# Splitting float32 weights and activations in a two-layer decoder trunk: GpSimd's share of the weights goes to VectorE, feature-major tiles are split two at a time, and the idle products at the layer norms have other forms

## The chip, the cores and the metric

The kernel runs on one core of a Trainium2 chip. The core has TensorE (PE, matrix products, weight loads shown apart as PEld), VectorE (DVE), ScalarE (ACT), GpSimd (POOL) and SyncE (SP, which here only issues DMAs). Each engine runs its own instructions in order and waits for the others by semaphores. The metric is device time in microseconds (us) of one execution; lower is better. TensorE's clock has two levels, 2.4 and 1.2 GHz; the profile calls the first a granted clock of 1.00 and the second 0.50.

## The reference

Two post-norm decoder layers over 256 tokens of width 2048, all in float32, cut to the parts that give the work its order:

```python
for layer in range(2):
    mixed = even_mixer(x, ...) if layer == 0 else odd_mixer(x, ...)   # x @ w_in, attention, y @ w_out
    x = layer_norm(ALPHA * x + mixed, ln1_g[layer], ln1_b[layer])
    hid = jax.nn.relu(x @ mlp_w1[layer])                               # 2048 -> 8192
    x = layer_norm(ALPHA * x + (hid * hid) @ mlp_w2[layer], ln2_g[layer], ln2_b[layer])
```

The even mixer is a sliding-window attention beside a mixture of dilated ones, the odd mixer a stick-breaking attention beside a latent attention. Some 395 MB of weights are read once each.

## The kernel before

**Split products.** A float32 product is made of three products of numbers in the type float32r: each operand is split into a high part (a cast) and a low part (the operand less its high part). In the text *hi* and *lo* are these parts.

**Weights.** The class `Stream` holds all weights in the order of their use, in *units* of at most 128 x 1024 numbers (two k-tiles of 512 columns, for the products that matter here). SP loads a unit into one of 6 buffers `raw`, at least 5 units ahead; `_split` makes `w_hi` (ACT, L128) and `w_lo` (L129), 3 units ahead of the product, in 4 buffers each. So ACT can cast a new unit only when PE has finished with the unit four places before it. At the program's start and after each layer norm (`self.shared = SHARED`, 10) the next ten units are cut at column 320: ACT casts the two pieces one after the other, DVE subtracts the first 320 columns and GpSimd the other 704 (or 544).

**Activations.** x is kept token-major in `x_res`. `transposed` makes the feature-major k-tiles on demand, two at a time (a *pair*): four transposes on PE into one bank (L506), then for each of the two tiles ACT's copy with gain and bias into `xfull` (L516 or L518), DVE's cast to the high part (L519) and DVE's subtraction for the low part (L520). `LazyTiles.need` calls it just ahead of the unit that uses the pair: PE's order is pair 0, pair 1, unit 0, pair 2, unit 1, pair 3 and so on to pair 7, unit 6, unit 7. `xfull` has 3 buffers of 256 columns, and `join` (L345, L346), which adds the two sums of a bank, takes them too.

**The layer norm.** `layer_norm` ends a block: DVE adds the last column block to x for token tile 0, takes the moments, GpSimd raises the variance to the power -1/2 (`rs`, L559), and the same for token tile 1. PE has nothing to do then and `keep_clock` gives it products that nothing reads (L533). `z` (L584) normalizes x in place on DVE, 512 columns of one token tile at a time: the first block ahead of pair 0, the others behind pairs 0, 2 and 4. There are three such turns with products behind them, called here by layer and norm: turn (0, 1), turn (0, 2) and turn (1, 1). The last norm goes to the output.

**Work beside the products.** After each unit `pump` does one step of side work. One such step is in `x_new`, which multiplies the normed x by the gain and adds the bias; behind the norm with `ln == 2` it loads the gain and bias rows 128 columns at a time on GpSimd's queue (`g_row`, `b_row`), `lead` = 3 steps ahead in 4 buffers, and at the other norms whole (`gb_rows`). The first pumps of the program also issue the small loads (`gb`, `rg`, `masks`, `sinks`, L471) on GpSimd's queue.

The order on every engine is that in which the program is written; nothing reorders it.

Of the kernel before, what the change touches and what calls it, by code (L numbers as in the profile page):

```python
# [11 lines left out]
F32 = mybir.dt.float32  # L12
F32R = mybir.dt.float32r
# [5 lines left out]
P = 128  # L19
# [13 lines left out]
SHARED, DVE_PART = 10, 320  # L33
# [34 lines left out]
class Stream:  # L68
    """Weights in the order of their use: DMA ahead, split ahead into two float32r parts.
    For the next shared units GpSimd takes a share of the second part."""  # L70

    def __init__(self, k):
        self.k = k
        self.units = []
        self.nd = 0
        self.ns = 0
        self.nu = 0
        self.live = {}
        self.shared = SHARED
# [19 lines left out]
    def _split(self, upto):  # L99
        nc = self.k.nc  # L100
        while self.ns < min(upto, len(self.units)):
# [17 lines left out]
            else:  # L119
                m = n * width  # L120
                rv = raw.rearrange("p k c -> p (k c)")
                cuts = (0, m)
                if self.shared:
                    self.shared -= 1
                    cuts = (0, DVE_PART, m)
                pieces = [(hi[:, a:b], lo[:, a:b], rv[:, a:b]) for a, b in zip(cuts, cuts[1:])]
            for i, (h, l, r) in enumerate(pieces):
                nc.scalar.copy(h, r)  # L128
                (nc.gpsimd if i and perm is None else nc.vector).tensor_tensor(l, r, h.bitcast(F32), op=ALU.subtract)  # L129
# [14 lines left out]
class LazyTiles:  # L144
    """feature-major k-tiles that are made when a product comes near them"""
# [13 lines left out]
class Job:  # L159
    """one group of attention heads: scores, then stages of the weighting, then the values"""  # L160
# [11 lines left out]
class Trunk:  # L172
# [22 lines left out]
    # ---- work beside the products: one step per unit of weights  # L195
# [17 lines left out]
    def queue(self, job, u=None):  # L213
        """all heads; pattern u only, when the patterns come one by one"""
        if u is None:
            self.todo.extend((job, h, 0) for h in range(job.n))
        else:
            self.todo.extend((job, h, u) for h in range(job.n))
# [42 lines left out]
    def flip(self, job, h, u):  # L261
        """weights of a head (and pattern) to keys-major"""
# [40 lines left out]
    # ---- psum  # L303
# [3 lines left out]
    # ---- matrix products; xs: per k-tile (hi, lo) of [128, 256]  # L307
# [4 lines left out]
    def ws(self, xs, nkt, width, take, more=False):  # L312
        """weights stationary, feature-major result. Per 128 features one bank: the first 256 columns sum
        hi x hi, the other 256 the two cross terms; take(f, bank) is called when the sums of tile f are complete"""
# [26 lines left out]
    def join(self, out, bank, scale=1.0):  # L341
        """both sums of a bank, scaled by a power of two"""
        nc = self.nc
        t = self.small.tile([P, S], F32, name="xfull", bufs=3)
# [3 lines left out]
    def as_(self, xs, nkt, width, hold=0):  # L348
        """activations stationary: token-major result [128 tokens, width] for both token tiles;
        the last hold units of weights serve first the one token tile, then the other"""  # L350
# [35 lines left out]
    # ---- weights in the order in which the products below take them  # L386
# [58 lines left out]
    # ---- set-up  # L445
# [49 lines left out]
    def x_slot(self, k):  # L495
        return self.parts(self.res.tile([P, 2 * S], F32R, name=f"x{k}"))

    def transposed(self, ln, z=None):
        """x (token-major) to feature-major k-tiles, split; ln=(which, layer) applies its gain and bias"""
        nc = self.nc  # L500
        for kp in range(KT // 2):
# [6 lines left out]
            out = []  # L508
            for j in range(2):
                k = 2 * kp + j  # L510
                x = self.x_slot(k)
                xh, xl, _ = x
                src = pt[:, j * S:(j + 1) * S]
                full = self.small.tile([P, S], F32, name="xfull", bufs=3)
                if ln is None:
                    nc.scalar.copy(full, src)  # L516
                else:
                    nc.scalar.activation(full, src, AF.Identity, bias=self.gcol(*ln, k, 1), scale=self.gcol(*ln, k, 0))  # L518
                nc.vector.tensor_copy(xh, full)  # L519
                nc.vector.tensor_tensor(xl, full, xh.bitcast(F32), op=ALU.subtract)  # L520
                out.append(x)
# [6 lines left out]
    def keep_clock(self, n, t=None):  # L528
        """products that nothing takes, while the array waits, so that its clock is not halved"""
# [5 lines left out]
    # ---- residual sums and layer norm  # L535
# [17 lines left out]
    def rstd(self, var, n, eps, scale=1.0):  # L553
        """(var * scale + eps) ** -0.5"""
# [7 lines left out]
    def moments(self, last, stats):  # L562
        """the last column block into x, and per token tile the mean and 1/deviation"""
# [10 lines left out]
    def layer_norm(self, last, stats, ln, layer):  # L574
        nc = self.nc
        res = list(self.moments(last, stats))
        self.keep_clock(IDLE[1])
        self.w.shared = SHARED

        def z(c, parts=((0, 0, 512), (1, 0, 512))):  # L580
            for t, a, b in parts:
                mv, r = res[t]
# [3 lines left out]
        z(0, ((0, 0, 512), (1, 0, 256), (1, 256, 512)))  # L586
# [3 lines left out]
    def x_new(self, ln, layer):  # L590
        """the residual's copy of the normed x, token-major"""
        nc, a = self.nc, self.a
        g, b = a[f"ln{ln}_g"][layer], a[f"ln{ln}_b"][layer]
        w, lead = (512, 1) if ln == 1 else (128, 3)
# [33 lines left out]
    def final(self, last, stats):  # L628
        """the last layer norm, token-major, to the output"""
# [33 lines left out]
    # ---- attention  # L663
    def qk(self, sc, q, k):
        """q, k: feature-major [K, 256]; sc: q-block 0 in 128 columns, q-block 1 in 256"""
# [4 lines left out]
    def softmax(self, per, scale=1.0, sink=None):  # L670
        """three stages: maximum, exponentials, division"""
# [43 lines left out]
    # ---- layer 0 mixer  # L715
# [97 lines left out]
    def project(self, width, tag="qk", scale=1.0):  # L813
        """feature-major projection of x; tiles of [128, 2, 256] with two heads to a slice"""
# [5 lines left out]
    # ---- layer 1 mixer  # L820
# [327 lines left out]
```

## Time and profile before

| | us |
|---|---|
| median of 3 runs (2270.44 to 2273.03) | 2272.68 |
| span of the profiled execution, first to last instruction | 2269.1 |
| median less that span | 3.6 |
| PE busy, share of the span | 98% |
| DVE busy | 63% |
| ACT busy | 47% |
| POOL busy | 6% |
| mean granted clock of TensorE | 0.993 |

The profiled execution's own time is known by its span alone; what lies around the span (start and end of the program) is taken as the 3.6 us that part it from the median. Busy shares are means over the whole program; a busy PE may still run at its lower clock, which its products' durations show.

### The profile page before, as it was taken

The page shows a single profiled execution, that of the slowest core. Times are in us where ns is not written, and L with a number is a line of the kernel's source. Part 1 is how long each engine was busy: PE and PEld are TensorE (multiplying, and loading weights), DVE is VectorE, ACT ScalarE, POOL GpSimd, SP SyncE. Part 2 cuts the span into 40 slices and gives each one's busy share as a digit, 9 for nine tenths or more (in the row PEclk, how much of TensorE's full clock was granted, in tenths as well). Part 3 has the DMA queues.
Part 4 walks back from the last instruction along what each step waited for, and adds up shares of the span by engine and source line. Part 5 has one row for each costly group of instructions (what it writes and reads, how often), then busy time and mean ns, then how long its engine had stood idle before and what let it go on. Part 6 is the DMA issues. An engine that isn't in the chain of part 4 may idle for free. (4 is left out here: it accounts for less than half of the span.)

```text
span 2269.1 us, 30281 instructions
## 1 busy us (share of the span) xinstructions
PE 2228.8 (98%) x11633; PEld 1857.5 (82%) x11633; DVE 1435.0 (63%) x1967; ACT 1064.9 (47%) x1573; POOL 132.4 (6%) x125
## 2 busy tenths in 40 slices
PE   8999999999999999999999999999999999999997
PEld 7878787788888888888878878777888888888885
DVE  6766455785455556556567797978655655554655
ACT  4554344355345345345444575735534534443542
POOL 3000000120000000000024101003000000000001
PEclk9999999999999999999999999999999999999998
DMA  7445454465656665665658544355666566656553
GB/s 248 140 121 150 130 166 142 139 209 191 193 178 195 194 187 181 198 187 177 202 144 223 160 135 135 128 170 177 233 193 193 175 207 180 194 193 187 186 193 104
DMA packets 224322, 399.09 MB, mean 176 GB/s; under 512 B 12778, under 2 KB 56512, under 8 KB 223408
## 3 DMA queue, kind: packets, MB, share of 16 engines
q1 hardware_dynamic: 221760, 387.30, 54.6%
q0 software_dynamic: 2416, 9.84, 1.6%
q8 instruction: 91, 1.49, 0.3%
q14 instruction: 55, 0.45, 0.1%
HBM read 395.00 MB, written 2.10 MB: 175 GB/s over the span
## 5 line engine op out<-in xcount | busy, mean ns | idle before, releaser
L129 DVE TENSOR_TENSOR w_lo<-raw,w_hi 128x1024 fp32r<-128x1024 f32 (+3 forms) x748 | 879.0, 1188 | 589.9 <-ACT w_hi L128 583.0
L128 ACT CAST w_hi<-raw 128x1024 fp32r<-128x1024 f32 (+2 forms) x788 | 763.0, 986 | 777.2 <-PE acc L381 453.6
L333 PE MATMUL acc<-x,w_hi 128*128 128x512 f32 x1824 | 661.0, 405 | 12.4 <-DVE x L520 11.6
L334 PE MATMUL acc<-x,w_lo 128*128 128x256 f32 x1824 | 514.5, 282 | 0.0
L333 PEld LDWEIGHTS acc<-x,w_hi 128*128 128x128 f32 x1824 | 345.9, 190 | 106.7 <-DVE x L520 14.8
L381 PE MATMUL acc<-w_hi,h_lo 128*128 128x512 f32 x1016 | 399.3, 393 | 0.0
L380 PE MATMUL acc<-w_lo,h_hi 128*128 128x512 f32 x1016 | 398.0, 392 | 0.0
L379 PE MATMUL acc<-w_hi,h_hi 128*128 128x512 f32 x1016 | 395.6, 389 | 0.0
L334 PEld LDWEIGHTS acc<-x,w_lo 128*128 128x128 f32 x1824 | 348.0, 191 | 1.1 <-POOL w_lo L129 0.5
L380 PEld LDWEIGHTS acc<-w_lo,h_hi 128*128 128x128 f32 x1016 | 190.8, 188 | 43.2
L379 PEld LDWEIGHTS acc<-w_hi,h_hi 128*128 128x128 f32 x1016 | 190.7, 188 | 42.4
L381 PEld LDWEIGHTS acc<-w_hi,h_lo 128*128 128x128 f32 x1016 | 190.9, 188 | 39.5
L333 PE MATMUL sc<-x,w_hi 128*128 128x512 f32 x512 | 186.1, 397 | 0.0
L334 PE MATMUL sc<-x,w_lo 128*128 128x256 f32 x512 | 143.6, 281 | 0.0
L379 PE MATMUL acc<-w_hi,x 128*128 128x256 f32 (+2 forms) x400 | 137.3, 343 | 3.9 <-DVE x L519 3.8
L380 PE MATMUL acc<-w_lo,x 128*128 128x256 f32 (+2 forms) x400 | 133.4, 333 | 0.1
L381 PE MATMUL acc<-w_hi,x 128*128 128x256 f32 (+2 forms) x400 | 133.3, 333 | 0.0
L333 PEld LDWEIGHTS sc<-x,w_hi 128*128 128x128 f32 x512 | 96.1, 188 | 23.5
L559 POOL TENSOR_TENSOR rs<-ve,mhalf 128x1 f32<-128x1 f32 (+1 forms) x10 | 6.6, 659 | 1849.8 <-DVE ve L557 1843.8
L345 ACT ACTIVATE xfull<-acc 128x256 f32<-128x256 f32 x130 | 49.8, 384 | 127.0 <-PE acc L334 107.7
L334 PEld LDWEIGHTS sc<-x,w_lo 128*128 128x128 f32 x512 | 96.7, 189 | 0.0
L333 PE MATMUL o<-x,w_hi 128*128 128x512 f32 x256 | 96.0, 397 | 0.0
(194 smaller groups left out, 2376.1 us busy)
## 6 DMA issues: line engine op xcount, KB each, us to landing
raw<-in_mlp_w SPq DMA_DIRECT2D x512, 512.0 KB, 4.1
raw<-in_even_w_in SPq DMA_DIRECT2D x92, 512.0 KB, 4.0
raw<-in_odd_w_in SPq DMA_DIRECT2D x56, 512.0 KB, 4.4
raw<-in_odd_w_out SPq DMA_DIRECT2D x32, 512.0 KB, 3.7
raw<-in_even_w_out SPq DMA_DIRECT2D x24, 512.0 KB, 3.7
gb_rows<-in_ln_g POOLq DMA_DIRECT2D x3, 1024.0 KB, 6.7
gb_rows<-in_ln_b POOLq DMA_DIRECT2D x3, 1024.0 KB, 8.6
raw<-in_odd_w_uq SPq DMA_DIRECT2D x8, 384.0 KB, 3.6
```

The source lines that it names most:

```text
L128: nc.scalar.copy(h, r)
L129: (nc.gpsimd if i and perm is None else nc.vector).tensor_tensor(l, r, h.bitcast(F32), op=ALU.subtract)
L333: nc.tensor.matmul(banks[f], hi[:, c:c + P], both, start=first, stop=False, skip_group_check=True)
L334: nc.tensor.matmul(banks[f][:, S:2 * S], lo[:, c:c + P], xh, start=False, stop=last, skip_group_check=True)
L345: nc.scalar.activation(t, bank[:, S:2 * S], AF.Copy, scale=scale)
L379: nc.tensor.matmul(outs[t], xh[:, ts], hi[:, c:c + width], start=first, stop=False, skip_group_check=True)
L380: nc.tensor.matmul(outs[t], xh[:, ts], lo[:, c:c + width], start=False, stop=False, skip_group_check=True)
L381: nc.tensor.matmul(outs[t], xl[:, ts], hi[:, c:c + width], start=False, stop=last, skip_group_check=True)
L559: nc.gpsimd.tensor_tensor(r[:, :n], ve[:, :n], self.mhalf[:, :n], op=ALU.pow)
```

## The change

GpSimd takes no part of the split: `SHARED` and `DVE_PART` go, each unit is one cast on ACT and one subtraction on DVE. The two tiles of a pair lie in one buffer, and one cast and one subtraction on DVE serve both; at the program's start ACT's copy is one for both too. `xfull` becomes 2 buffers of 512 columns, of which `join` and `latents` use half. In place of nine products of the identity at a layer norm, `stay_warm` issues products of a resident x tile in a form of its own for each turn. `z` does token tile 0 of its second block ahead of token tile 1 of the first. `lead` for the rows of `x_new` goes from 3 to 2, with 3 buffers.

```diff
-                cuts = (0, m)
-                if self.shared:
-                    self.shared -= 1
-                    cuts = (0, DVE_PART, m)
-                pieces = [(hi[:, a:b], lo[:, a:b], rv[:, a:b]) for a, b in zip(cuts, cuts[1:])]
-            for i, (h, l, r) in enumerate(pieces):
+                pieces = [(hi[:, :m], lo[:, :m], raw.rearrange("p k c -> p (k c)"))]
+            for h, l, r in pieces:
                 nc.scalar.copy(h, r)
-                (nc.gpsimd if i and perm is None else nc.vector).tensor_tensor(l, r, h.bitcast(F32), op=ALU.subtract)
+                nc.vector.tensor_tensor(l, r, h.bitcast(F32), op=ALU.subtract)
...
-        t = self.small.tile([P, S], F32, name="xfull", bufs=3)
+        t = self.small.tile([P, 2, S], F32, name="xfull", bufs=2)[:, 0, :]
...
+            out = [self.x_slot(2 * kp), self.x_slot(2 * kp + 1)]
+            pair = self.x_pair.rearrange("p (j h s) -> p j h s", j=2, h=2)
+            full = self.small.tile([P, 2, S], F32, name="xfull", bufs=2)
+            if ln is None:
+                nc.scalar.copy(full, pt.rearrange("p (j s) -> p j s", j=2))
+            else:
+                for j in range(2):
+                    k = 2 * kp + j
+                    nc.scalar.activation(full[:, j, :], pt[:, j * S:(j + 1) * S], AF.Identity,
+                                         bias=self.gcol(*ln, k, 1), scale=self.gcol(*ln, k, 0))
+            nc.vector.tensor_copy(pair[:, :, 0, :], full)
+            nc.vector.tensor_tensor(pair[:, :, 1, :], full, pair[:, :, 0, :].bitcast(F32), op=ALU.subtract)
...
+    def stay_warm(self, where):
+        nc, w = self.nc, self.x_pair[:, 0:512]
+        if where == (0, 1):
+            o = self.ps.tile([P, 512], F32, name="pt")
+            for _ in range(6):
+                nc.tensor.matmul(o[0:64, :], w[:, 0:64], w, start=True, stop=True, skip_group_check=True)
+            for _ in range(3):
+                nc.tensor.matmul(o[:, 0:384], w[:, 0:P], w[:, 0:384], start=True, stop=True, skip_group_check=True)
+        elif where == (0, 2):
+            os = [self.ps.tile([P, 512], F32, name=n) for n in ("pt", "o")]
+            for i in range(8):
+                nc.tensor.matmul(os[i % 2], w[:, 0:P], w, start=True, stop=True, skip_group_check=True)
+        else:
+            o = self.ps.tile([P, 512], F32, name="pt")
+            b = w.bitcast(BF16)
+            for _ in range(8):
+                nc.tensor.matmul(o, b[:, 0:P], b[:, 0:512], start=True, stop=True, skip_group_check=True)
...
-        self.keep_clock(IDLE[1])
-        self.w.shared = SHARED
+        self.stay_warm((layer, ln))
...
-        z(0, ((0, 0, 512), (1, 0, 256), (1, 256, 512)))
+        done = set()
+        z(0, ((0, 0, 512),))
+        z(1, ((0, 0, 512),))
+        z(0, ((1, 0, 256), (1, 256, 512)))
...
-        w, lead = (512, 1) if ln == 1 else (128, 3)
+        w, lead = (512, 1) if ln == 1 else (128, 2)
```

What this does to DVE's order at turn (0, 1), from the first normalization on. Before:

```order
L584 TENSOR_SCALAR x_res<-x_res,mv,rs 128x512
L584 TENSOR_SCALAR x_res<-x_res,mv,rs 128x256 x2
L519 CAST x_4076<-xfull 128x256
L520 TENSOR_TENSOR x_4076<-xfull,x_4076 128x256
L519 CAST x_4081<-xfull 128x256
L520 TENSOR_TENSOR x_4081<-xfull,x_4081 128x256
L584 TENSOR_SCALAR x_res<-x_res,mv,rs 128x512 x2
L129 TENSOR_TENSOR w_lo<-raw,w_hi 128x320 x2
L519 CAST x_4114<-xfull 128x256
L520 TENSOR_TENSOR x_4114<-xfull,x_4114 128x256
```

The same place on DVE after the change (L598 is `z`, L513 and L514 the cast and the subtraction of a pair, L121 the low part of a unit):

```order
L598 TENSOR_SCALAR x_res<-x_res,mv,rs 128x512 x2
L598 TENSOR_SCALAR x_res<-x_res,mv,rs 128x256 x2
L513 CAST x_4016<-xfull 128x2x256
L514 TENSOR_TENSOR x_4016<-xfull,x_4016 128x2x256
L598 TENSOR_SCALAR x_res<-x_res,mv,rs 128x512
L121 TENSOR_TENSOR w_lo<-raw,w_hi 128x1024 x2
L513 CAST x_4045<-xfull 128x2x256
L514 TENSOR_TENSOR x_4045<-xfull,x_4045 128x2x256
```

One normalization of 512 columns has moved ahead, four instructions of a pair have become two, and each subtraction of a weight unit has its full 1024 columns.

GpSimd's order from the program's start, before:

```order
L1144 UNCONDITIONAL_BRANCH
L129 ISA
L129 TENSOR_TENSOR w_lo<-raw,w_hi 128x704 x10
L471 DMA gb<-in_ln_g 16x2x128
L471 DMA gb<-in_ln_b 16x2x128
L471 DMA gb<-in_ln_g 16x2x128
L471 DMA gb<-in_ln_b 16x2x128
L471 DMA rg<-in_odd_q_norm_g 4x128
L471 DMA rg<-in_odd_kv_norm_g 2x128
L471 DMA masks<-in_m_even 128x1536
```

And after:

```order
L1161 UNCONDITIONAL_BRANCH
L463 DMA gb<-in_ln_g 16x2x128
L463 DMA gb<-in_ln_b 16x2x128
L463 DMA gb<-in_ln_g 16x2x128
L463 DMA gb<-in_ln_b 16x2x128
L463 DMA rg<-in_odd_q_norm_g 4x128
L463 DMA rg<-in_odd_kv_norm_g 2x128
L463 DMA masks<-in_m_even 128x1536
```

The ten subtractions that stood ahead of the small loads are gone; nothing that waits for another engine's work stands ahead of them now.

## Rows read from the trace of the kernel before

**Rows 1.** The waits of TensorE, longest first: who waited for whom, us in total, times, longest.

```profile
PE acc L333 <- DVE x L520: 11.6, 9, 3.6
PE acc L379 <- DVE x L519: 3.8, 1, 3.8
```

**Rows 2.** The timeline of the program's start: start us, us, engine, line, operation, and in brackets the idle time before it and who ended it.

```profile
7.28 1.11 PE L506 MATMUL sc<-ident,x_res 128*128 128x128 f32 x4 [0.88 <-DMA x_res<-in_x]
...
18.28 1.80 DVE L519 CAST x<-xfull 128x256 fp32r<-128x256 f32 x1
...
19.89 3.54 POOL L129 TENSOR_TENSOR w_lo<-raw,w_hi 128x704 fp32r<-128x704 f32 x2
...
22.05 0.47 PE L333 MATMUL acc<-x,w_hi 128*128 128x512 f32 x1 [1.38 <-DVE x L520]
...
24.19 0.77 PE L333 MATMUL acc<-x,w_hi 128*128 128x512 f32 x1 [1.56 <-DVE x L520]
...
24.97 0.63 PE L333 MATMUL acc<-x,w_hi 128*128 128x512 f32 x1
...
28.83 0.39 PE L333 MATMUL acc<-x,w_hi 128*128 128x512 f32 x1
...
38.78 0.50 PE L333 MATMUL acc<-x,w_hi 128*128 128x512 f32 x1 [0.35 <-DVE x L520]
```

**Rows 3.** The transposes of pairs 3, 4, 5 and 7 at the program's start, in PE's timeline. They mark how far the units have come.

```profile
16.81 0.60 PE L506 MATMUL sc<-ident,x_res 128*128 128x128 f32 x4
20.07 0.60 PE L506 MATMUL sc<-ident,x_res 128*128 128x128 f32 x4
28.04 0.60 PE L506 MATMUL sc<-ident,x_res 128*128 128x128 f32 x4
...
35.01 0.60 PE L506 MATMUL sc<-ident,x_res 128*128 128x128 f32 x4
```

**Rows 4.** The timeline of turn (0, 1): the idle products, ACT's two copies of pair 0, unit 0's first product, DVE's second and third `z`, GpSimd's subtractions, DVE's, unit 1's first product, the transposes of pair 3, unit 7's first product.

```profile
431.48 2.17 PE L533 MATMUL pt<-ident 128*128 128x128 f32 x18
...
435.53 1.02 ACT L518 ACTIVATE xfull<-sc,gbc 128x256 f32<-128x256 f32 x2 [8.28 <-PE sc L506]
...
437.03 0.47 PE L333 MATMUL acc<-x,w_hi 128*128 128x512 f32 x1 [0.21 <-ACT w_hi L128]
...
437.47 2.39 DVE L584 TENSOR_SCALAR x_res<-x_res,mv,rs 128x512 f32<-128x512 f32 x2
...
437.71 5.57 POOL L129 TENSOR_TENSOR w_lo<-raw,w_hi 128x704 fp32r<-128x704 f32 x3 [3.27 <-ACT w_hi L128]
...
439.78 3.85 DVE L129 TENSOR_TENSOR w_lo<-raw,w_hi 128x320 fp32r<-128x320 f32 x2
...
444.35 0.79 PE L333 MATMUL acc<-x,w_hi 128*128 128x512 f32 x1 [3.57 <-DVE x L520]
...
449.65 0.94 PE L506 MATMUL sc<-ident,x_res 128*128 128x128 f32 x4
...
468.05 0.50 PE L333 MATMUL acc<-x,w_hi 128*128 128x512 f32 x1 [0.38 <-DVE x L520]
```

**Rows 5.** Stretches of turn (0, 1): from:to and length, busy us and instructions of PE, PEld, DVE, ACT and POOL, then the granted clock, the share of the DMA engines' time and GB/s.

```profile
442.00:444.00 2.00, 0.00 (x0) 0.00 (x0) 1.97 (x3) 0.00 (x0) 1.28 (x1) 0.88 0.50 122
444.00:446.00 2.00, 1.65 (x5) 1.40 (x6) 1.93 (x7) 0.56 (x1) 0.00 (x0) 0.50 0.80 210
```

**Rows 6.** First products of units 0, 1 and 7 in turn (0, 2), then in turn (1, 1).

```profile
1167.24 0.47 PE L379 MATMUL acc<-w_hi,x 128*128 128x512 f32 x1
...
1174.95 0.79 PE L379 MATMUL acc<-w_hi,x 128*128 128x512 f32 x1 [3.84 <-DVE x L519]
...
1197.55 0.39 PE L379 MATMUL acc<-w_hi,x 128*128 128x512 f32 x1
...
1532.32 0.47 PE L333 MATMUL acc<-x,w_hi 128*128 128x512 f32 x1 [0.20 <-ACT w_hi L128]
...
1539.64 0.79 PE L333 MATMUL acc<-x,w_hi 128*128 128x512 f32 x1 [3.61 <-DVE x L520]
...
1561.97 0.50 PE L333 MATMUL acc<-x,w_hi 128*128 128x512 f32 x1 [0.35 <-DVE x L520]
```

**Rows 7.** Durations on DVE: groups by form (busy us, mean ns), and for two lines ns min/median/max over all their instructions.

```profile
L129 DVE TENSOR_TENSOR w_lo<-raw,w_hi 128x1024 fp32r<-128x1024 f32 x682 | 831.3, 1230 | 574.7 <-ACT w_hi L128 570.4
L1076 DVE TENSOR_TENSOR h_lo<-sq,h_hi 128x512 fp32r<-128x512 f32 x64 | 44.3, 693 | 7.0 <-DVE sq L1075 0.5
L519 DVE CAST x<-xfull x64: 279/288/1807, 6.0 to 1561.8; 128x256 fp32r<-128x256 f32 x64
L584 DVE TENSOR_SCALAR x_res<-x_res,mv,rs x27: 407/541/1980, 433.5 to 1551.9; 128x512 f32<-128x512 f32 x21, 128x256 f32<-128x256 f32 x6
```

**Rows 8.** DMA at the program's start: a stretch (columns as in rows 5), and the load of the masks with KB and us from issue to landing.

```profile
14.00:16.00 2.00, 2.00 (x14) 1.73 (x13) 1.30 (x5) 1.77 (x5) 0.76 (x2) 1.00 1.05 407
...
masks<-in_m_even POOLq DMA_DIRECT2D x1, 768.0 KB, 4.6
```

**Rows 9.** The rows of gain and bias behind turn (0, 2): the landings of those issued from 1206.1 to 1216 us, and DVE's waits for them.

```profile
b_row<-in_ln_b POOLq DMA_DIRECT2D x5, 64.0 KB, 7.3
...
DVE x_res L617 <- DMA b_row<-in_ln_b: 3.0, 3, 1.6
```

**Rows 10.** ACT's longest waits for a buffer of `xfull` at a join.

```profile
ACT xfull L345 <- DVE relu L346: 2.2, 2, 1.1
```

More of the change, by code (lines that the diff above doesn't have):

```diff
@@ L32 @@
 IDLE = (6, 9, 4, 2)
-SHARED, DVE_PART = 10, 320
 def alibi(n):
@@ L78, in __init__ @@
         self.live = {}
-        self.shared = SHARED
     def add(self, src, shape, perm=None):
@@ L120, in _split @@
                 m = n * width
-                rv = raw.rearrange("p k c -> p (k c)")
-                cuts = (0, m)
-                if self.shared:
-                    self.shared -= 1
-                    cuts = (0, DVE_PART, m)
-                pieces = [(hi[:, a:b], lo[:, a:b], rv[:, a:b]) for a, b in zip(cuts, cuts[1:])]
-            for i, (h, l, r) in enumerate(pieces):
+                pieces = [(hi[:, :m], lo[:, :m], raw.rearrange("p k c -> p (k c)"))]
+            for h, l, r in pieces:
                 nc.scalar.copy(h, r)
-                (nc.gpsimd if i and perm is None else nc.vector).tensor_tensor(l, r, h.bitcast(F32), op=ALU.subtract)
+                nc.vector.tensor_tensor(l, r, h.bitcast(F32), op=ALU.subtract)
             self.units[self.ns] = (hi, lo, n, width)
@@ L495, in x_slot @@
     def x_slot(self, k):
-        return self.parts(self.res.tile([P, 2 * S], F32R, name=f"x{k}"))
+        if k % 2 == 0:
+            self.x_pair = self.res.tile([P, 4 * S], F32R, name=f"x{k // 2}")
+        return self.parts(self.x_pair[:, (k % 2) * 2 * S:(k % 2 + 1) * 2 * S])
     def transposed(self, ln, z=None):
@@ L507, in transposed @@
                                         self.x[:, t, k * P:(k + 1) * P], self.ident)
[L508 to L521, printed above, removed]
+            out = [self.x_slot(2 * kp), self.x_slot(2 * kp + 1)]
[10 more added lines that the diff above has]
+            nc.vector.tensor_tensor(pair[:, :, 1, :], full, pair[:, :, 0, :].bitcast(F32), op=ALU.subtract)
             if kp == 0:
@@ L576, in layer_norm @@
         res = list(self.moments(last, stats))
-        self.keep_clock(IDLE[1])
-        self.w.shared = SHARED
+        self.stay_warm((layer, ln))
         def z(c, parts=((0, 0, 512), (1, 0, 512))):
             for t, a, b in parts:
+                if (t, c, a) in done:
+                    continue
+                done.add((t, c, a))
                 mv, r = res[t]
@@ L913, in latents @@
                     lh, ll, _ = lat
-                    full = self.small.tile([P, S], F32, name="xfull", bufs=3)
+                    full = self.small.tile([P, 2, S], F32, name="xfull", bufs=2)[:, 0, :]
                     nc.scalar.activation(full, src, AF.Copy, scale=g)
```

## The prediction

> **What bounds the kernel now.** I read the page first: PE is busy for 98% of the span, so time can be won only where PE waits or runs at its lower clock. The waits of PE come next [rows 1]: nearly all of its waiting is for DVE's cast or subtraction of an x tile (11.6 + 3.8 us). The timelines show where: at the program's start [rows 2] and once in each turn, each time as one gap of 3.6 to 3.8 us between unit 0 and unit 1 [rows 4, 6].
>
> The reader is to see two things there. First, why DVE is late. A cast of 256 columns takes 288 ns in the median, but up to 1807 ns [rows 7]; the long ones run while GpSimd's subtraction is under way (18.28 and the stretch from 19.89 [rows 2]). In turn (0, 1) GpSimd's three run from 437.71 to 443.28, and in that time DVE's two `z` take 2.39 us in place of two at 541 ns, and its two 320-column subtractions 3.85 us, more than the 2 x 1230 ns that two whole ones take elsewhere [rows 4, 7]. GpSimd's help costs DVE more than it spares. Second, each gap is paid twice: behind it the clock is granted at 0.50, 1.2 GHz [rows 5], and a product takes 0.63 us in place of 0.39 [rows 2]. In turn (0, 1) unit 1 lasts from 444.35 to 449.65 that way [rows 4].
>
> **Undisturbed pace.** From pair 3 to pair 4 at the start PE needs 20.07 - 16.81 = 3.26 us for a unit and four transposes [rows 3]. I take that for every unit, about 2.86 for the unit and 0.4 for the transposes (an estimate: their row shows 0.60, but its end overlaps the next product).
>
> **The change, turn (0, 1).** ACT's second copy of pair 0 still ends at 436.55 [rows 4]. The pair's cast of 512 columns is in no row: `z` goes from 407 to 541 ns when its columns double, so 288 + 130 = 0.42 us; twice the single cast, 0.58, is the upper end. Its two halves lie apart in the output, which no row prices; I take 0.42, as `z` is the nearest row. The subtraction is 0.69 [rows 7]. The pair is ready at 437.7 and unit 0 starts at about 437.8, 0.77 later than before (437.03), because it now needs both tiles. DVE goes on with one `z` (0.54), two whole `w_lo` (2.46) and pair 1 (1.11): ready at 441.8. PE is through with unit 0 and its transposes at 441.06 and waits 0.75, in place of 3.57 us. Six more units, the last without transposes, take 6 x 3.26 - 0.4 = 19.16: unit 7 starts at 461.0 instead of 468.05 [rows 4]. **7.05 us won.**
>
> Behind that DVE must keep up. Per unit it has 1.23 + 0.42 + 0.69 = 2.34 us, and 1.08 more of `z` in two of the units, against 3.26. The tight path is ACT's cast (about 1.05, an estimate from two half-unit copies) once PE has left a unit, then these three: 3.4 us, against 3.66 until PE needs the pair. So the 704 columns that DVE takes over cost nothing, hidden behind PE's products; with 0.58 for the cast 0.1 us of cover is left, and if it goes, each unit waits 0.1 to 0.2 us, up to 4 us in all four places.
>
> **Turns (1, 1) and (0, 2).** The same shift, 0.77 for unit 0 and 4.05 to unit 1, puts unit 1 of turn (1, 1) at 1537.1 and unit 7 at 1556.3 instead of 1561.97: **5.7 us**. In turn (0, 2) the first product of a unit reads the high part only, so unit 1 follows about 4.6 us behind the old start of unit 0, at 1171.9, and unit 7 starts at 1191.0 instead of 1197.55 [rows 6]: **6.5 us**.
>
> **The start.** Undisturbed, pair 7 would follow pair 4 by 3 x 3.26, at 29.85 instead of 35.01 [rows 3], and the wait of 0.35 ahead of unit 7 [rows 2] goes: 5.5 us. But GpSimd's small loads now stand at the head of its queue and go out in the first 5 us, where they waited for ten subtractions before. They are some 0.85 MB, 768 KB of it masks, and the DMA engines are full there, 407 GB/s at a share of 1.05 [rows 8]: all that lands later is late by up to 0.85 / 0.407 = 2.1 us. That is on the path, since PE waits for x ahead of pair 1 (7.28 [rows 2]) and the weights follow it. Between 0 (if the x chunk lands first) and 2.1 I take 1.7: **3.8 us won.**
>
> The Trainium skill bears on this ("DMA: Bandwidth & Descriptors", section "Queues, rings and completion order"): each DMA engine goes round robin between the queues that have work for it, so a load on GpSimd's queue does not stand behind SP's. By that rule the x chunk would feel nearly the whole 2.1 us, and the start would win 3.4. No row here shows the two queues together under load.
>
> **Row loads.** With 3 buffers in place of 4, the load for step c + 3 goes out when step c has been added. Five landings took 7.3 us, and DVE already waited 3.0 us [rows 9]; the next `w_lo` stands behind that wait. Three steps then take at least 7.3 + 0.6 = 7.9 us (0.6 for handing the buffer over, an estimate), 2.6 a step, against 2.86 a unit: it just fits, but the first few loads come in late behind the norm of the latent queries, and PE will meet a late `w_lo` once. I take 0.7 us, from 0 to 4 (ten steps 0.4 too long). Turn (0, 2) is left with **5.8 us**.
>
> **What costs nothing.** The idle products' new forms are in no row. At the pace of the old ones (2.17 us for nine) eight take 1.9 and end ahead of the transposes; at twice that they would push them by 1.3 us a turn. I take 0, since a 512-column product lasts 0.39 us with its end overlapped. `z` of the second block fills the time in which DVE waits for `rs`. `join` with two buffers: ACT waited only 2.2 us with three [rows 10], and behind ACT stand casts made 3 units ahead, about 9 us of cover.
>
> **Sum.** 3.8 + 7.05 + 5.8 + 5.7 = 22.35 us off the profiled execution: 2269.1 becomes 2246.8. What lies around the span, 3.6, stays: **2250.3 us**, against the median of 2272.68.
>
> **Rivals.**
> *The clock falls in the turns.* PE idles 0.21 us ahead of unit 0 before [rows 4] and about 1 us after the change, behind idle products that end no later; at the start two gaps of 1.38 and 1.56 us with 0.7 us of products between them were followed by half speed [rows 2]. Against it: in the old turn (0, 1) PE had 5.5 us of idle products, transposes and small holes, and unit 0's first product still took 0.47 us [rows 4], not the 0.77 to 0.79 of one that starts at half speed. If it falls, a unit takes 2.3 us more at 0.63 for 0.39 and the wait of 0.75 vanishes under it, some 2 us a turn: 16.4 us won, 2256.3. The Trainium skill speaks for this one ("TensorE: Matmul & The Clock Gate", Part 4, PE-mode transpose): a transpose does not count as a busy array does. By that rule the transposes of pairs 0 and 1 would not hold the clock, which no row here tests. Chance 0.15.
>
> *DVE or the row loads hold PE.* Both upper ends above, 4 us each less the 0.7 counted: 15 us won, 2257.6. The 0.25 us of cover speaks for it, the mean load of DVE (2.7 of 3.26) against. Chance 0.10.
>
> *It doesn't do what it says.* If DVE's long operations had another cause than GpSimd, the pair's cast and subtraction would stay at up to 1.8 us each, DVE would need 1.23 + 3.6 a unit, and 4 x 6 units at 1.6 over PE's 3.26 would give back all and 15 us more: 2288. The median of 288 ns wherever GpSimd is idle speaks against it. Chance 0.02.
>
> *Slower: the joins.* With two buffers of `xfull`, ACT's third join of a unit waits for DVE's first, and if that holds PE at the 32 groups of four joins in the two MLPs (two layers, four quarters, four blocks), the gain is gone at 22.35 / 32 = 0.70 us a group; at 1.23, one whole `w_lo` ahead of DVE's first join, it would be 17 us slower, 2290. Against it stands the cover named above. Chance 0.03.
>
> **How the numbers follow.** The forecast has 0.68, with a range of its own from 2245 to 2254 (start 2 us either way, turns 3). The other 0.02 is for a gain that mostly fails without one of these causes. The range 2245.5 to 2258.5 takes in the forecast, the clock and DVE's upper ends. A measurement of this kernel can tell about 0.2%, 4.5 us, from no change: faster 0.92, same 0.03, slower 0.05.
>
> **What would show it.** In the changed profile: no cast on DVE far over 0.6 us at these four places; PE's waits for DVE there of under 1 us each; no stretch at 0.50 between unit 0 and unit 7 of a turn; unit 7 at 35.0, and in each turn some 30 us behind the idle products' start; GpSimd's load of the masks issued in the first 5 us. The prediction is wrong if the clock falls ahead of unit 0, if PE waits for `w_lo` behind turn (0, 2), or if the start's x lands more than 2 us later.

## The result, and the profile after

| | before | after |
|---|---|---|
| median of 4 runs, us | 2271.56 | 2248.38 |
| span of the profiled execution, us | 2269.1 | 2246.6 |
| PE busy | 98% | 99% |
| DVE busy | 63% | 63% |
| POOL busy | 6% | 3% |

The changed kernel takes 0.9902 of the time before (95% interval 0.9890 to 0.9914): 23.2 us less by the medians, 22.5 by the profiled spans. The forecast was 22.35 us less, and 2250.3 us.

TensorE's waits after the change, longest first (columns as in [rows 1]; L501 are the transposes, L325 and L326 the products of high and low weights, L371 those of turn (0, 2)):

```profile
PE acc L325 <- DVE x L514: 4.0, 7, 1.1
PE sc L501 <- DVE x_res L598: 3.9, 6, 0.7
...
PE acc L326 <- DVE w_lo L121: 0.6, 1, 0.6
...
PE acc L371 <- DVE x L513: 0.2, 1, 0.2
```

The 11.6 and 3.8 us of waiting for x tiles are 4.0 and 0.2, and none of these waits is longer than 1.1 us. Turn (0, 1) after the change, to be read against [rows 4], and three stretches of it against [rows 5] (from:to and length, PE's busy us and instructions, granted clock, share of the DMA engines, GB/s):

```profile
426.18 1.54 PE L534 MATMUL pt<-x 128*64 128x512 f32 x6
427.56 0.68 PE L536 MATMUL pt<-x 128*128 128x384 f32 x3
...
430.32 1.02 ACT L511 ACTIVATE xfull<-sc,gbc 128x256 f32<-128x256 f32 x2 [8.36 <-PE sc L501]
...
431.37 0.43 DVE L513 CAST x<-xfull 128x512 fp32r<-128x512 f32 x1 [1.37 <-ACT xfull L511]
...
432.67 0.47 PE L325 MATMUL acc<-x,w_hi 128*128 128x512 f32 x1 [1.06 <-DVE x L514]
...
432.90 2.35 DVE L121 TENSOR_TENSOR w_lo<-raw,w_hi 128x1024 fp32r<-128x1024 f32 x2
...
436.37 0.50 PE L325 MATMUL acc<-x,w_hi 128*128 128x512 f32 x1 [0.25 <-DVE x L514]
...
455.85 0.50 PE L325 MATMUL acc<-x,w_hi 128*128 128x512 f32 x1
```

```profile
430.00:432.00 2.00, 1.61 (x15) 1.00 0.76 209
432.00:434.00 2.00, 1.33 (x7) 1.00 1.01 410
434.00:436.00 2.00, 2.00 (x14) 1.00 0.99 418
```

The gap ahead of unit 1 has gone from 3.57 to 0.25 us, the clock is granted in full throughout, and unit 7 starts 29.67 us behind the idle products' start, where it was 36.57. DVE's times over the whole program (ns, least, median, most; L513 and L514 split a pair, L598 is `z`, L121 makes `w_lo`; compare [rows 7]):

```profile
L513 DVE CAST x<-xfull x32: 418/421/428, 6.1 to 1536.1; 128x512 fp32r<-128x512 f32 x32
...
L514 DVE TENSOR_TENSOR x<-xfull,x x32: 691/693/694, 6.6 to 1536.6; 128x512 fp32r<-128x512 f32 x32
...
L598 DVE TENSOR_SCALAR x_res<-x_res,mv,rs x27: 395/541/544, 428.2 to 1527.8; 128x512 f32<-128x512 f32 x21, 128x256 f32<-128x256 f32 x6
...
L121 DVE TENSOR_TENSOR w_lo<-raw,w_hi x748: 282/1225/2320, 7.2 to 2215.9; 128x1024 fp32r<-128x1024 f32 x179, 128x128 fp32r<-128x128 f32 x4, 128x864 fp32r<-128x864 f32 x2, 128x768 fp32r<-128x768 f32 x2
```

No cast, no subtraction of a pair and no `z` is stretched any more. Five subtractions of `w_lo` still are, at 1249 to 1389 us in the odd mixer: they take 1.8 to 2.3 us, each beside an addition of GpSimd's there (L956), which both kernels have. In the kernel before they took as long. Idle products and unit 7's first product in turns (0, 2) and (1, 1), and unit 7 at the start ([rows 6] and [rows 2]):

```profile
1149.59 0.40 PE L540 MATMUL pt<-x 128*128 128x512 f32 x1
...
1178.40 0.39 PE L371 MATMUL acc<-w_hi,x 128*128 128x512 f32 x1
...
1507.55 1.90 PE L545 MATMUL pt<-x 128*128 128x512 bf16 x8
...
1537.31 0.50 PE L325 MATMUL acc<-x,w_hi 128*128 128x512 f32 x1
...
34.54 0.50 PE L325 MATMUL acc<-x,w_hi 128*128 128x512 f32 x1
```

**Where the 22.5 us went.** To compare all kernels alike I cut each span at the same marks: a turn runs from DVE's second `BATCH_NORM_AGGREGATE` of its norm (427.83 in turn (0, 1) after, 1.65 us behind the idle products' start) to the transposes of pair 7; the start runs to its own pair 7. All in us, from PE's and DVE's timelines; the rest of the span is what lies between.

| kernel | start | turn (0, 1) | turn (0, 2) | turn (1, 1) | span |
|---|---|---|---|---|---|
| before | 35.01 | 31.14 | 30.57 | 29.79 | 2269.1 |
| after | 31.03 | 24.51 | 23.95 | 24.61 | 2246.6 |
| e1, before without the share | 30.84 | 24.60 | 23.62 | 24.57 | 2246.0 |
| e2, after with the share | 32.39 | 31.36 | 28.89 | 30.09 | 2267.8 |
| e3, GpSimd subtracts for nobody | 34.05 | 32.56 | 23.81 | 31.47 | 2270.9 |
| e4, GpSimd copies for nobody | 31.28 | 26.62 | 23.80 | 26.57 | 2252.0 |
| e12, GpSimd sets to zero for nobody | 28.95 | 24.51 | 23.92 | 24.51 | 2245.9 |
| e5, small loads late | 28.77 | 24.50 | 23.88 | 24.56 | 2240.8 |
| e6, no idle products ahead of `z` | 30.95 | 24.51 | 24.25 | 24.98 | 2243.8 |
| e7, none at all in the turns | 30.98 | 26.45 | 25.69 | 25.87 | 2249.3 |
| e11, transposes in their place | 30.91 | 24.43 | 23.90 | 25.76 | 2241.8 |
| e8, rows one step ahead | 31.07 | 24.51 | 23.88 | 24.56 | 2249.1 |
| e9, first tile first | 31.71 | 23.39 | 22.74 | 23.53 | 2241.0 |
| e10, e9 with the loads late | 28.84 | 23.39 | 22.77 | 23.54 | 2237.1 |

From before to after the four stretches lose 3.98 + 6.63 + 6.62 + 5.18 = 22.41 us, and all that lies between them 0.1: the gain is where it was looked for. The long stretches between differ by 1 to 3 us from one execution to the next where no instruction is changed (behind turn (1, 1) 712.80 us after, 710.36 in e5), so small effects are read from the table, not from medians. The kernel before took 2271.97 us beside e1 to e4, 2270.32 beside e5 to e8 and 2268.30 beside e9 to e12, in place of 2271.56; the ratios below are each to the one beside it.

### The profile page after: what moved, and what is told of

Its sections match the earlier page's. It is cut to its first block, busy times and chain, and to the rows that moved or that the text cites. A ratio compares the mean times of both kernels' runs of the same rounds, so it can differ in the third digit from the quotient of the medians.

```text
span 2246.6 us, 30036 instructions
## 1 busy us (share of the span) xinstructions
PE 2216.6 (99%) x11604; PEld 1847.6 (82%) x11604; DVE 1406.8 (63%) x1903; ACT 1060.7 (47%) x1525; POOL 62.0 (3%) x85
## 4 chain that ended last, share of the span: by engine, by line
PE 64%; issue 30%; DVE 4%; ACT 1%; DMA 1%; POOL 0%; SPq 0%; POOLq 0%; DVEq 0%; ACTq 0%
PE acc L325 14%; PE acc L371 9%; PE acc L373 9%; PE acc L372 9%; PE acc L326 7%; PE sc L325 3%; PE sc L326 2%; PE o L325 2%; PE pt L325 2%; PE pt L259 1%; PE o L278 1%; PE sc L685 1%; DVE w_lo L121 1%; PE sc L684 1%; PE o L326 1%
## 5 line engine op out<-in xcount | busy, mean ns | idle before, releaser
L121 DVE TENSOR_TENSOR w_lo<-raw,w_hi 128x1024 fp32r<-128x1024 f32 (+2 forms) x748 | 891.5, 1204 | 600.0 <-ACT w_hi L120 595.0
L325 PE MATMUL acc<-x,w_hi 128*128 128x512 f32 x1824 | 654.0, 402 | 4.3 <-DVE x L514 4.0
L326 PE MATMUL acc<-x,w_lo 128*128 128x256 f32 x1824 | 512.3, 281 | 0.6 <-DVE w_lo L121 0.6
L325 PEld LDWEIGHTS acc<-x,w_hi 128*128 128x128 f32 x1824 | 343.3, 188 | 94.4 <-issue 6.6
L371 PE MATMUL acc<-w_hi,h_hi 128*128 128x512 f32 x1016 | 394.4, 388 | 0.0
L326 PEld LDWEIGHTS acc<-x,w_lo 128*128 128x128 f32 x1824 | 345.2, 189 | 1.4 <-DVE w_lo L121 0.9
L371 PEld LDWEIGHTS acc<-w_hi,h_hi 128*128 128x128 f32 x1016 | 190.7, 188 | 42.7
L325 PE MATMUL sc<-x,w_hi 128*128 128x512 f32 x512 | 186.7, 399 | 0.0
L326 PE MATMUL sc<-x,w_lo 128*128 128x256 f32 x512 | 143.8, 281 | 0.0
L371 PE MATMUL acc<-w_hi,x 128*128 128x256 f32 (+2 forms) x400 | 136.4, 341 | 0.3 <-DVE x L513 0.2
L325 PEld LDWEIGHTS sc<-x,w_hi 128*128 128x128 f32 x512 | 96.2, 188 | 23.9
L326 PEld LDWEIGHTS sc<-x,w_lo 128*128 128x128 f32 x512 | 96.7, 189 | 0.0
L325 PE MATMUL o<-x,w_hi 128*128 128x512 f32 x256 | 96.3, 399 | 0.0
L325 PE MATMUL pt<-x,w_hi 128*128 128x512 f32 x256 | 96.2, 399 | 0.0
```

What stands on the lines that cost most here:

```text
L121: nc.vector.tensor_tensor(l, r, h.bitcast(F32), op=ALU.subtract)
L325: nc.tensor.matmul(banks[f], hi[:, c:c + P], both, start=first, stop=False, skip_group_check=True)
L326: nc.tensor.matmul(banks[f][:, S:2 * S], lo[:, c:c + P], xh, start=False, stop=last, skip_group_check=True)
L371: nc.tensor.matmul(outs[t], xh[:, ts], hi[:, c:c + width], start=first, stop=False, skip_group_check=True)
```

## Experiments: is it GpSimd's share, and is it its reading?

**e1: before, without the share alone.**

```diff
-SHARED, DVE_PART = 10, 320
+SHARED, DVE_PART = 0, 320
```

> The kernel before with GpSimd's share of the split taken away and nothing else: tiles are still split one by one, idle products, z order and row buffers are the old ones. Theory A (GpSimd's subtractions hold DVE up, and that is the whole of it): nearly all of the 23.2 us are won, 2247 to 2253; per unit DVE needs 1.23 + 1.38 us for the four instructions of a pair in place of 1.11, which just fits beside PE's 3.26, so at most 0.3 us a unit goes back; unit 0 of a turn starts some 0.8 us earlier than with whole pairs; no cast on DVE over 0.6 us. Theory B (the gain needs the pairs, the order of z or the idle products): less than half is won, 2260 or more.

Measured: 2246.44 us, 0.9892 of before (0.9870 to 0.9914). Theory B falls: this one number is the whole gain, and the pairs, the order of `z`, the other idle products and the row buffers add nothing that these times show. Tiles split one by one cost nothing, and unit 0 starts 5.55 us behind the idle products (426.40 to 431.95) in place of 6.49.

```profile
L519 DVE CAST x<-xfull x64: 284/287/296, 5.8 to 1536.3; 128x256 fp32r<-128x256 f32 x64
```

The cast that took up to 1807 ns [rows 7] takes at most 296.

**e2: the share put back into the changed kernel.**

```diff
-                pieces = [(hi[:, :m], lo[:, :m], raw.rearrange("p k c -> p (k c)"))]
-            for h, l, r in pieces:
+                rv = raw.rearrange("p k c -> p (k c)")
+                cuts = (0, m)
+                if self.shared:
+                    self.shared -= 1
+                    cuts = (0, 320, m)
+                pieces = [(hi[:, a:b], lo[:, a:b], rv[:, a:b]) for a, b in zip(cuts, cuts[1:])]
+            for i, (h, l, r) in enumerate(pieces):
                 nc.scalar.copy(h, r)
-                nc.vector.tensor_tensor(l, r, h.bitcast(F32), op=ALU.subtract)
+                (nc.gpsimd if i and perm is None else nc.vector).tensor_tensor(l, r, h.bitcast(F32), op=ALU.subtract)
...
+        self.w.shared = 10
```

> The changed kernel with GpSimd's share put back at the start and after each norm (columns 320 on, ten units), all else as changed. Theory A: DVE's long casts and z come back (up to 1.8 us), the gap of 3 to 4 us ahead of unit 1 and the half clock behind it too, and the small loads go out late again: 2266 to 2274. Theory B: pairs and the new order keep most of the gain, 2248 to 2256.

Measured: 2269.08 us, 0.9991 (0.9981 to 1.0001) of before. The long instructions are back (a pair's cast up to 1885 ns, `z` up to 2049), and PE's waits with them:

```profile
PE acc L331 <- DVE x L520: 13.4, 13, 3.1
```

**e3: GpSimd works for nobody.**

```diff
             for h, l, r in pieces:
                 nc.scalar.copy(h, r)
                 nc.vector.tensor_tensor(l, r, h.bitcast(F32), op=ALU.subtract)
+            if self.shared and perm is None and self.k.spare is not None:
+                self.shared -= 1
+                hb = hi.bitcast(F32)
+                t = self.k.spare.tile([P, 704], F32, name="unread", bufs=1)
+                nc.gpsimd.tensor_tensor(t, hb[:, 320:1024], hb[:, 320:1024], op=ALU.subtract)
...
+        self.w.shared = 10
```

> The changed kernel; at the start and in turns (0, 1) and (1, 1) (not in (0, 2)) GpSimd subtracts 704 columns of w_hi from themselves into a tile that nobody reads, once for each of ten units. DVE does its whole work as in the changed kernel and takes nothing from GpSimd, so no data is waited for. Theory A (GpSimd's reading itself holds DVE up): DVE's casts and subtractions grow to 1.7 us and more while GpSimd's 1.77 us instruction runs, PE waits for DVE ahead of unit 1, the clock falls behind it, and 14 us or more are lost: 2262 to 2285. Theory C (DVE was late because it waited for data, or ACT's casts in two pieces): the casts stay at 0.43, 2248 to 2250.

Measured: 2273.25 us, 1.0011 (1.0001 to 1.0021) of before. Nobody waits for `unread`, yet turns (0, 1) and (1, 1) grow by 8.05 and 6.86 us, and turn (0, 2), which has none of it, is as it was. So neither a wait for GpSimd's data nor ACT's cast in two pieces made DVE late. The place, in turn (0, 1):

```profile
436.71 2.86 POOL L127 TENSOR_TENSOR unread<-w_hi 128x704 f32<-128x704 f32 x2 [3.17 <-ACT w_hi L121]
436.75 1.61 DVE L605 TENSOR_SCALAR x_res<-x_res,mv,rs 128x512 f32<-128x512 f32 x1
...
441.11 1.91 POOL L127 TENSOR_TENSOR unread<-w_hi 128x704 f32<-128x704 f32 x1 [1.53 <-ACT w_hi L121]
441.72 1.58 DVE L519 CAST x<-xfull 128x512 fp32r<-128x512 f32 x1
...
444.07 0.79 PE L331 MATMUL acc<-x,w_hi 128*128 128x512 f32 x1 [3.64 <-DVE x L520]
```

The cast that starts at 441.72 ends at 443.30, which is GpSimd's end (443.02) and 0.28 us more, where a whole cast takes 0.42: it waits for most of its time, then runs. The gap of 3.64 us and the product of 0.79 behind it are like those of the kernel before, 3.57 and 0.79 [rows 4].

**e4 and e12: a copy, then a write that reads next to nothing**, in the place of e3's subtraction.

```diff
-                nc.gpsimd.tensor_tensor(t, hb[:, 320:1024], hb[:, 320:1024], op=ALU.subtract)
+                nc.gpsimd.tensor_copy(t, hb[:, 320:1024])
```

is e4, and e12 has in that place

```diff
+                nc.gpsimd.tensor_copy(t[:, 0:1], hb[:, 320:321])
+                nc.gpsimd.memset(t, 0.0)
```

> As the run before, but GpSimd copies 704 columns (one input) in place of a subtraction with two. Theory A1 (what counts is how long GpSimd's instruction lasts, whatever it reads): DVE's instructions wait for the copy's whole length; the loss goes with its duration against 1.77 us, 2253 to 2280. Theory A2 (only two inputs hold DVE up): 2248 to 2250.

> The changed kernel; at the start and in turns (0, 1) and (1, 1) GpSimd copies one column of w_hi and then sets a tile of 704 columns that nobody reads to zero, ten times. It reads next to nothing and writes as much as in the runs with its copies and subtractions. If any long instruction of GpSimd holds DVE up, DVE's cast, z and subtraction grow as with the copy: some 2 us a turn lost. If only its reads do, the subtractions of w_lo stay at 1.23 us and the loss is under 0.5 us a turn, with at most the casts and z longer.

Measured: e4 2253.83 us, 0.9927 (0.9909 to 0.9944); e12 2246.62 us, 0.9902 (0.9887 to 0.9916). Against the changed kernel the copy costs 2.0 to 2.1 us in each of its turns, the write nothing. First the copy, then the write:

```profile
438.31 0.69 DVE L520 TENSOR_TENSOR x<-xfull,x 128x512 fp32r<-128x512 f32 x1
438.39 1.25 POOL L127 COPY unread<-w_hi 128x704 f32<-128x704 f32 x1 [2.66 <-ACT w_hi L121]
438.92 1.79 DVE L122 TENSOR_TENSOR w_lo<-raw,w_hi 128x1024 fp32r<-128x1024 f32 x1
```

```profile
8.34 0.69 POOL L128 MEMSET unread<- 128x704 f32 x1
8.46 0.85 DVE L520 CAST x<-xfull 128x512 fp32r<-128x512 f32 x1 [0.22 <-ACT xfull L514]
...
431.34 0.96 POOL L128 MEMSET unread<- 128x704 f32 x1
...
431.60 2.35 DVE L122 TENSOR_TENSOR w_lo<-raw,w_hi 128x1024 fp32r<-128x1024 f32 x2
```

In the first, GpSimd's copy (0.77 us alone) starts inside DVE's subtraction and ends at 439.64, and DVE's next one is 0.56 us longer than its 1.23: they take turns. In the second, the two subtractions under the write keep their 2.35 us, while the one cast of the 32 that starts inside a write, at 8.46, takes 0.85 and ends 0.28 us behind it; no `z` starts inside one. Theory A stands, and A1 and A2 are both too simple: a read of GpSimd, of one input or two, holds back casts, `z` and subtractions alike; a write held back the cast that started inside it, and no subtraction.

The Trainium skill states this in "SBUF — State Buffer", section "Who interferes with whom": one pair of ports is shared and goes to whoever starts first for the whole instruction; a DVE instruction with two SBUF inputs is held up by a GpSimd instruction that reads, not by one that only writes. The rows above agree on each point.

## Experiments: the start

**e5: the small loads on SP's queue, behind the weights of units 14 to 17.**

```diff
             for dst, src in some:
-                nc.gpsimd.dma_start(dst, src)
+                nc.sync.dma_start(dst, src)
```

> The changed kernel with the small loads (gain and bias columns, masks, sinks) issued by SP, in the order of its weight loads behind those of units 10 to 13, in place of GpSimd's queue in the first 5 us. Theory (the prediction's term: 1.7 us of the start go to these loads): ACT's waits for raw at 13 to 20 us shrink, unit 7's first product comes at 32.8 to 33.3 in place of 34.54, 2246 to 2247.5. Rival (the weights are late by the full DMA engines alone): unit 7 at 34.3 or later, 2248.4. That the masks come some 25 us later costs nothing by both, since the first use of them lies behind the first projections.

Measured: 2242.97 us, 0.9876 (0.9861 to 0.9891). In the trace the loads go out behind units 14 to 17 (units counted from 0), at 28.34 to 40.29 us, not behind 10 to 13. Unit 7 starts at 32.27 in place of 34.54, so these loads cost 2.27 us, more than the 1.7 counted; the time lies 3.0 us below what was expected. PE and the DMA engines in the changed kernel, then in e5 (columns as above):

```profile
20.00:24.00 4.00, 3.54 (x23) 1.00 1.05 409
24.00:28.00 4.00, 3.33 (x20) 1.00 1.05 392
...
28.00:29.00 1.00, 1.00 (x9) 1.00 1.02 391
```

```profile
20.00:24.00 4.00, 3.70 (x23) 1.00 1.05 401
24.00:28.00 4.00, 4.00 (x26) 1.00 0.87 332
...
27.00:28.00 1.00, 1.00 (x8) 1.00 0.33 125
```

With the loads ahead the DMA engines are still full at 28 to 29 us, in e5 no longer at 27 to 28: some 2 us. PE stands still for 1.13 us of the 8 from 20 to 28, in e5 for 0.30. e12 shows the same unasked: there the ten copies stand ahead of the loads in GpSimd's queue, as the subtractions did before, and the masks go out at 35.56 in place of 4.58; its start takes 28.95 us. In unit 0 e12 and the changed kernel ran at half clock (granted 0.57 and 0.58 over 8 to 12 us) and e5 did not, yet e12 and e5 end within 0.2 us of each other; after, e1, e6, e7, e8 and e11, whose loads go out early, end at 30.84 to 31.07 (e9 at 31.71). The end of the start goes by the bytes ahead of the weights, not by the clock.

## Experiments: the clock, the rows, the order

**e6, e7 and e11: the idle products.**

```diff
-        self.stay_warm((layer, ln))
```

That is e6. e7 has this as well:

```diff
-            if kp == 0:
-                self.keep_clock(IDLE[3] if ln is None else IDLE[2])
+            if kp == 0 and ln is None:
+                self.keep_clock(IDLE[3])
```

and e11 adds to e7:

```diff
+            elif kp == 0:
+                o = self.ps.tile([P, 512], F32, name="pt")
+                for i in range(11):
+                    nc.tensor.transpose(o[:, (i % 4) * P:(i % 4 + 1) * P], self.ident, self.ident)
```

> The changed kernel without the idle products ahead of the z of the three turns; the four products of the identity behind pair 0 stay. Theory (the prediction's: transposes and small holes hold the clock well enough once the idle products have held it): without them PE idles some 3 us more ahead of pair 0 and the clock falls to half in unit 0; about 2 us a turn lost, 2252 to 2257. Rival (they do nothing): the clock stays at 1.00, 2248.4.

> As the run before, and without the four products of the identity behind pair 0 as well, so that between the block ahead and unit 0 PE does the transposes of two pairs alone. If transposes count for the clock, as much is lost as in the run before; if they do not, unit 0 starts at half speed for longer and 1 to 3 us more are lost than there.

> The changed kernel without the idle products of the turns, and with eleven transposes of the identity in place of the four products of the identity behind pair 0. The run without idle products but with those four kept the clock in turn (0, 1) and lost 0.3 us in the other two; the run without both lost 1.3 to 1.9 us a turn at half clock. If transposes hold the clock as products do, this one is like the former (turns of 24.2 to 25.0 us); if they do not count, like the latter (25.7 to 26.5 us).

Measured: e6 2246.04 us, 0.9892 (0.9877 to 0.9907); e7 2251.54 us, 0.9912 (0.9897 to 0.9927); e11 2246.96 us, 0.9902 (0.9883 to 0.9920). Turn (0, 1) of e7, then of e11:

```profile
430.41 0.98 PE L501 MATMUL sc<-ident,x_res 128*128 128x128 f32 x7 [0.61 <-DVE x_res L597]
433.35 0.77 PE L325 MATMUL acc<-x,w_hi 128*128 128x512 f32 x1 [1.95 <-DVE x L514]
```

```profile
430.79 1.36 PE L520 MATMUL pt<-ident 128*128 128x128 f32 x11
...
433.35 0.47 PE L325 MATMUL acc<-x,w_hi 128*128 128x512 f32 x1 [0.75 <-DVE x L514]
```

The theory of e6 fell: without `stay_warm` turn (0, 1) is the same and the others lose 0.30 and 0.37 us, where the clock fell ahead of unit 0 and was back at its start or soon behind. With `stay_warm` gone, what counts are the four products behind pair 0; whether `stay_warm` would do without them no run shows. Without both, PE idles 1.95 us ahead of unit 0 in turn (0, 1), which then runs at 1.2 GHz (granted clock 0.50 over 432 to 436 us, 0.77 us for the first product), and 1.3 to 1.9 us a turn are lost. e11 is split: with transposes in their place the clock stayed at 1.00 in turns (0, 1) and (0, 2); in turn (1, 1) it had fallen in the 2.45 us of idling ahead of the first transpose and unit 0 began at half speed. Each turn ran once, so why the three differ is open.

**e8: the rows one step ahead.**

```diff
-        w, lead = (512, 1) if ln == 1 else (128, 2)
+        w, lead = (512, 1) if ln == 1 else (128, 1)
```

> The changed kernel with the rows of gain and bias behind turn (0, 2) loaded one step ahead in 2 buffers, in place of two steps in 3. By the prediction's sum (a landing of 5 to 7 us, a step of 2.86 us) each of 16 steps then lasts 6 to 8 us if DVE has to wait for it, w_lo stands behind that wait and PE is late for it: up to 16 x 3 = 48 us lost, 2260 to 2296. Rival (the cover of 3 units of w_lo hides it, as with 3 buffers): 2248 to 2251.

Measured: 2250.98 us, 0.9911 (0.9895 to 0.9928). DVE's wait for the rows and PE's for `w_lo` behind turn (0, 2), in e8:

```profile
DVE x_res L634 <- DMA b_row<-in_ln_b: 9.7, 13, 2.2
...
PE acc L372 <- DVE w_lo L121: 4.5, 3, 2.4
```

In the changed kernel DVE waits 3.8 us there (3.0 before, [rows 9]) and PE not at all. The time falls within the rival's range, not the theory's. The chain that the prediction feared is real all the same, but begins one buffer lower: the stretch from turn (0, 2) to the next norm grows by 5.6 us (334.00 to 339.62), about a tenth of the worst case.

**e9 and e10: a version beyond both.** In the turns, pair 0 is split tile by tile again, and pair 1 comes ahead of the weights of units 2 and 3; e10 has e5's loads too.

```diff
-            nc.vector.tensor_copy(pair[:, :, 0, :], full)
-            nc.vector.tensor_tensor(pair[:, :, 1, :], full, pair[:, :, 0, :].bitcast(F32), op=ALU.subtract)
+            for a, b in ((0, 1), (1, 2)) if kp == 0 and ln is not None else ((0, 2),):
+                nc.vector.tensor_copy(pair[:, a:b, 0, :], full[:, a:b, :])
+                nc.vector.tensor_tensor(pair[:, a:b, 1, :], full[:, a:b, :], pair[:, a:b, 0, :].bitcast(F32), op=ALU.subtract)
...
+            if kt == 0 and self.w.nu:
+                self.near(xs, kt + 2, 1024 // width, nkt)
             hi, lo, n, wd = self.w.next(ahead=self.split_ahead - end)
```

> The changed kernel with two things moved in the three turns: DVE splits pair 0 one tile at a time, and pair 1's transposes, copies, cast and subtraction come ahead of the split of units 2 and 3. Theory (a turn's length is set by DVE's chain up to unit 0 and then by PE's 3.26 us a unit): unit 0 starts 1.0 us earlier, since it no longer waits for the second tile's copy, and unit 1 without its wait of 0.25; 1.2 us a turn, 3.5 us in all, 2244 to 2246. Rival (units 2 and 3 come late instead, because ACT's casts stand behind pair 1's copies): unit 2 waits as long as unit 0 has won, 2248.4.

> The run before together with the small loads behind units 10 to 13 on SP's queue. The two lie in different stretches and should add: 2.3 us at the start and 3.5 us in the turns below the changed kernel, 2242 to 2243.

Measured: e9 2242.35 us, 0.9883 (0.9868 to 0.9897); e10 2239.70 us, 0.9872 (0.9855 to 0.9889). Each turn is 1.1 to 1.2 us shorter, as expected, and with the late loads the start 2.2. The times lie 1.7 and 2.3 us below what was expected, in runs beside which the kernel before took 3.3 us less too. The two edits of e9 were not tried apart. Unit 0 of turn (0, 1) in e9, 5.64 us behind the idle products, and with a wait of 0.21 in place of 1.06:

```profile
427.59 1.54 PE L539 MATMUL pt<-x 128*64 128x512 f32 x6
...
433.23 0.47 PE L327 MATMUL acc<-x,w_hi 128*128 128x512 f32 x1 [0.21 <-DVE x L519]
```

## Why the prediction was right, step by step

**The cause** was as read: GpSimd's subtraction stretches DVE, DVE holds PE, PE's clock falls. e1 takes the chain away by that alone; e2 and e3 bring it back, the latter with no data in it.

**The sum.** By unit 7 the four terms are 4.24 + 6.90 + 6.60 + 5.44 = 23.2 us against 22.35, while the spans part by 22.5. That the total came within 0.2 us is in part luck: errors of up to 0.8 us in a term offset each other, and the long stretches vary by more.

**Turns.** By unit 7 behind the idle products, turn (0, 1) won 6.90 us (7.05 forecast), turn (0, 2) 35.41 - 28.81 = 6.60 (6.5 before the row loads were taken off), turn (1, 1) 35.20 - 29.76 = 5.44 (5.7). Unit 0 came 0.94 us later, not 0.77: 0.09 of that is ACT's copies, at 4.14 us behind the idle products in place of 4.05 (4.06 in e1), so moving `z` of the second block ahead was not quite free. Unit 1 waited 0.25, not 0.75. The pair's cast took 0.42 as taken, its apart-lying halves cost nothing, and the 704 columns stayed hidden behind PE's products.

**The start** came out at 4.24 won for 3.8, through two errors that offset each other, which is luck. The undisturbed start was put at pair 7 = 29.85, counted on from pair 4 as if all ahead of it were undisturbed; e5 and e12 show 28.77 and 28.95. Their unit 7 starts at 32.27 and 32.49, where it was 38.78 [rows 2], so the term of 5.5 should have been 6.3 to 6.5. The small loads cost 2.1 to 2.3 us, not 1.7, and not by way of pair 1's x: its transposes began at 7.01 (7.28 before, 7.49 in e5), and it was the loads behind that came late. Two of ACT's waits for them, after the change:

```profile
13.27 1.05 ACT L120 CAST w_hi<-raw 128x1024 fp32r<-128x1024 f32 x1 [3.58 <-DMA raw<-in_even_w_in]
...
17.23 1.05 ACT L120 CAST w_hi<-raw 128x1024 fp32r<-128x1024 f32 x1 [1.47 <-DMA raw<-in_even_w_in]
```

In e5 the same two casts start at 11.32 and 15.25. From issue to landing, the weights that SP issued at 3.70 us and the masks that GpSimd issued at 4.58, then the same weights in e5 (KB, us):

```profile
raw<-in_even_w_in SPq DMA_DIRECT2D x1, 512.0 KB, 9.6
masks<-in_m_even POOLq DMA_DIRECT2D x1, 768.0 KB, 7.9
```

```profile
raw<-in_even_w_in SPq DMA_DIRECT2D x1, 512.0 KB, 7.6
```

The masks landed at 12.46, ahead of weights that SP had issued 0.9 us before them, and these came 2 us later than in e5. That agrees with the Trainium skill's round robin ("DMA: Bandwidth & Descriptors", section "Queues, rings and completion order"), by which a DMA engine serves in turn the queues that have work for it. The upper end of the prediction's sum, 2.1 us, was nearer in size than the 1.7 taken. The x chunk that it named, issued at 2.16 us, did not feel the masks; the next one, issued at 3.19, took 8.2 us to land in place of 6.8.

**Row loads** were put at 0.7 us and cost nothing (334.00 us from turn (0, 2) to the next norm, 334.05 before); e8 shows their price with a buffer less. **Joins**: ACT's waits for DVE there are 0.8 and 0.6 us in all (2.2 the longest entry before, [rows 10]), behind casts that are made ahead.

**The rivals.** The clock did not fall in the turns: it was granted in full in all three. At the start it did, for which the prediction has no term: unit 0's products take 0.63 us there in both kernels. e12 beside e5 shows no cost of it. e7 shows that the rival's price of 2 us a turn was about right (1.3 to 1.9). What stood against it were the idle products; the working did not tell the four behind pair 0 from the others, and e6 against e7 shows that these four alone keep most of the loss away. DVE held PE nowhere beyond the first two units of a turn. One reading was off and carries little: the products between the two gaps at the start last 0.6 us (22.05 to 24.19, less the wait of 1.56 [rows 2]), not 0.7.

## To carry to other kernels

Read a helper's price in the durations of the engine beside it: where one line's instructions have a median and a maximum six times apart, look for what runs on GpSimd in the long ones, and test it with work that nobody waits for. At a program's start with full DMA engines every load that is not needed yet costs its own bytes; find out what had held it back before taking that away. Ahead of a first product, split the first tile alone and leave later weights for behind it (e9).

## What the runs showed of the hardware

- GpSimd is held up too: its copy of a single column of `w_hi` in e12 takes 1.24 us beside a subtraction of DVE of 1.23 that began 0.03 us earlier; the least is 0.19. Its write of 704 columns there takes 0.86 to 0.98 us where a cast or `z` of DVE had begun before it, and 0.69 else.
- With transposes alone TensorE's granted clock stayed at 1.00 in two of e11's three turns. The Trainium skill ("TensorE: Matmul & The Clock Gate", Part 4, PE-mode transpose) says that they do not count as a busy array does. e7, with transposes only, lost the clock in all three turns; e11, with eleven more and 1.2 us less idling, did not in two. The rule as it stands is not borne out there, and these runs don't settle it: e6, with the four products, lost the clock for a while in two turns.
